# An S5 scan layer on one core: the last quarter's odd columns in VectorE's scan, its lag products and early halves ahead of the scan's end

## The chip, the cores and the metric

The kernel runs on one core of a Trainium2 chip. The metric is the device time of one execution in microseconds; three executions of the kernel before took 1019.77, 1023.63 and 1024.74 us, so the median is 1023.63 us. Engines are named as in the profile: PE is TensorE (PEld its weight loads), DVE is VectorE, ACT is ScalarE, POOL is GpSimd, SP is SyncE, which here only issues DMAs.

## The reference

One layer works on 1024 latent tokens and 256 context tokens of width 1024, all in fp32. The mixer is a bidirectional S5: 64 groups of 16 channels, each with 64 complex states per direction.

```python
def run(u, h0):
    bu = jnp.einsum('lgh,gnh->lgn', u.astype(F32), b_bar)
    bu = bu.at[0].add(lam_bar * h0)
    a = jnp.broadcast_to(lam_bar, bu.shape)
    _, h = lax.associative_scan(_linear_combine, (a, bu), axis=0)
    return jnp.einsum('lgn,ghn->lgh', h, c_mat).real, h[-1]
...
def out(y, h):
    y = y.reshape(h.shape).astype(h.dtype) + d_skip * h
    g = jax.nn.gelu(y)
    return g * jax.nn.sigmoid(g @ w_glu + b_glu)
...
x = x + m_l[2][:, None] * y_l
h_l = modulate(rms_norm(x, norm_ffn[i]), m_l[3][:, None], m_l[4][:, None])
x = x + m_l[5][:, None] * swiglu(h_l, ffn_w1[i], ffn_w3[i], ffn_w2[i])
return rms_norm(x, norm_final)
```

Forward and backward direction are summed. Norms, shifts, scales and gates surround the mixer and a SwiGLU FFN of hidden width 2816; the output is the latent stream.

## The kernel before, in words

**Chunks.** Tokens are cut into chunks of eight: 32 context chunks, then 128 latent ones. Per chunk PE sums the inputs into one state contribution (`sums`), so the recurrence runs over 160 columns. The states lie in the tile `ra` in four quarters `STQ[q]`; a quarter is `[160 columns, 2 (real, imaginary), 16]`, 20.125 KB per partition, and `STE` is all four seen as one. A quarter belongs to two units; unit k has eight groups, and `16 q + 8 (k % 2)` is its place among the states, four places for the forward direction and four for the backward one. Column 31 is the last context state, columns 32 to 159 are latent. "Early" is the first 64 latent chunks, "late" the rest.

**The scan** (line 839) is a chain on VectorE over all quarters at once. Its first loop takes 32 steps of two columns (32 odd columns of the early half), the second 63 steps of one column through the late half. A step is two products and two additions (lines 637 and 846), each addition reading what is just written. The even-numbered places of the early half that the first loop jumps over are filled in separately with one product pair and two additions (`rot_ops`): for quarters 0 and 2 by `fill_ops` on VectorE, one such instruction after each of the step's two additions (`one`), for quarters 1 and 3 by `fill` on POOL (`F10 F11` and `F30 F31`, 16 instructions each pair).

**What each unit needs on PE.** `k_mats` (K, two per quarter, line 802) multiplies lag by lag the kernels of chunk-internal inputs; two ACT copies and two ACT DMAs bring its result to DRAM (`KD_`). `toeplitz` (T, line 824) is a DMA from there, issued by SP, that lays the lags out as a matrix in `KQ`; unit k uses loads 2k and 2k+1, which need both K of the quarter. `x_mm` multiplies the unit's inputs with the two halves of that matrix (line 945). `states_mm` (line 914) multiplies the chunk-start states with C: forward states straight from `STQ`, backward ones from a turned copy (`turned`: R for the early half, Z for the late). For units 0 to 5, P does `x_mm` and the early half into PSUM, Y copies that into `Y` with ACT, and after the scan N does the late half, D adds it to `Y` on VectorE, H is the GELU on ACT. Units 6 and 7 are done whole behind the scan: z turns all 128 columns, Q does `x_mm` and `states_all` (line 925), and H reads PSUM.

**The order** is written out by hand in two strings, `PROG1` (its PSUM pools are those of the scan) and `PROG2` (a new pool of eight banks `pe8` that lies over all of them). Each word is an operation and a number, and `run` (line 954) emits them one after the other; each engine executes its instructions in this order. C is a product of C with powers of lambda on POOL, summed by POOL (`E` in `HOWS`, line 30) or by PE and an ACT copy (`P`, line 669). A is the adaLN product, I and J turn the mixer's output and split it into two fp32r parts for the GLU, W and V split GLU weights, g starts GLU products, w, l, b and m are DMA loads on SP. Behind `PROG2` come the GLU units, the FFN and the final norm, almost all of it PE work.

Of the kernel before, what the change touches and what calls it, by code (L numbers as in the profile page):

```python
# [10 lines left out]
F32 = mybir.dt.float32  # L11
# [6 lines left out]
P = 128  # L18
# [5 lines left out]
T = 8  # L24
# [2 lines left out]
NS = 64  # L27
EPS = 1e-6
MAGIC = 12582912.0
HOWS = "PPPP PPEE PEEE EEEE"  # L30
ZEN = "VVSVSVSV"
PROG1 = ("A22 B0 A26 C02 G1 A30 A34 C03 A40 K0 A44 A48 C10 K1 L2 A54 G2 C11 A60 F10 C12 F11 C13 T0 T1 T2 T3 A64 M0 M1 K2 R0 P0 Y0 Y1 K3 L3 R1 C20 P1 Y2 Y3 T4 T5 G3 T6 T7 C21 C22 C23 K4 R2 P2 Y4 Y5 K5 R3 P3 Y6 Y7 T8 T9 T10 T11 C30 C31 R4 P4 Y8 Y9 C32 C33 R5 P5 Y10 Y11 M2 m0 F30 F31")
# [10 lines left out]
def s5_ffn_kernel(tc, a, out):  # L43
# [3 lines left out]
    with ctx:  # L47
# [776 lines left out]
        def toeplitz(u):  # L824

            q, gi = divmod(u, 4)
            rows = KD_[q][32 * gi:32 * gi + HC]
            n = 15 * HC
            src = bass.AP(rows.tensor, rows.offset, [[HC, T], [n, 4 * HC], [1, P]])
            SY.dma_start(KQ[u % 4], src)  # L830
# [64 lines left out]
        def turned(k, half, hs, eng):  # L895

            e = 8 * (k % 2) + 4
            n = 128 if half == 2 else 64
            c1 = 94 if half == 0 else 158
            src = STQ[k // 2][:, c1:c1 - n:-1, :, e:e + 4]  # L900
            if eng is S:
                S.copy(hs, src)
# [6 lines left out]
        def yview(k, gp):  # L909
            return Y[:, k].rearrange("p t (a e h) -> p e a t h", e=2, h=HC)[:, gp]  # L910

        def states_mm(k, pts, half, hs, start):

            for a_ in range(4):
                for ri in range(2):
                    for d in range(2):
                        cs_ = slice(64 * (half ^ d), 64 * (half ^ d) + 64)
                        c0 = 31 + 64 * half
                        for gp in range(2):
                            ps = slice(64 * gp, 64 * gp + 64)  # L920
                            st = hs[ps, :, ri, a_] if d else STQ[k // 2][ps, c0:c0 + 64, ri, 8 * (k % 2) + a_]
                            PE.matmul(flat(pts[gp][cs_, a_]), st, flat(CL[k // 2][ps, ri, d, 4 * (k % 2) + a_]),
                                      start=start and ri == 0, stop=ri == 1 and (start or a_ == 3))

        def states_all(k, pts, hs):

            for a_ in range(4):
                for ri in range(2):
                    for d in range(2):
                        for c in range(2):  # L930
                            cs_ = slice(64 * c, 64 * c + 64)
                            for gp in range(2):
                                ps = slice(64 * gp, 64 * gp + 64)
                                st = hs[ps, cs_, ri, a_] if d else STQ[k // 2][ps, 31 + 64 * c:95 + 64 * c, ri, 8 * (k % 2) + a_]
                                PE.matmul(flat(pts[gp][cs_, a_]), st, flat(CL[k // 2][ps, ri, d, 4 * (k % 2) + a_]),
                                          start=False, stop=a_ + ri + d == 5)

        def x_mm(k, pool):

            pts = [pool([4, T, HC]) for _ in range(2)]  # L940
            for a_ in range(4):
                for gp in range(2):
                    g = 2 * a_ + gp
                    kq = KQ[(2 * k + g // 4) % 4][:, g % 4].rearrange("p (t h) -> p t h", t=T)[:, ::-1]
                    PE.matmul(pts[gp][:, a_], U[:, 8 * k + g, 32:160], kq, start=a_ == 0, stop=False)
            return pts

        scan()
        inner = {}
        HSe = [view(r, kb, [64, 2, 4]) for r, kb in ((RC[3], 14), (RC[3], 12), (RC[3], 14), (RC[3], 12), (RA, 2), (RA, 0))]  # L950
        HSl = [view(RA, STB * (i // 3) + 4.125 + 2 * (i % 3), [64, 2, 4]) for i in range(6)]
        HSq = {6: view(RA, 0, [P, 2, 4]), 7: view(RA, STB, [P, 2, 4])}

        def run(prog):


            for w in prog.split():
# [2 lines left out]
                    ada(i)  # L960
                elif op == "M":
                    mod_cols(i)
                elif op == "k":
                    KT[i] = [pe8([15 * HC]) for _ in range(2)]
                    for kv in KT[i]:
                        V.memset(kv, 0.0)
                elif op == "K":
                    k_mats(*divmod(i, 2), KT.get(i) or [kt, zeros(pw([15 * HC])) if i < 4 else pm[:, 0:15 * HC]])
                elif op == "L":
                    cs_load(i, S)  # L970
                elif op == "G":
# [6 lines left out]
                    for f in cl_ops(q, part, cts[q][part], HOW[q][part]):  # L978
                        f()
                elif op == "F":  # L980
                    fill(*divmod(i, 10), *((RW, 0) if i >= 30 else (RC[3], 12)))
                elif op == "T":
                    toeplitz(i)
                elif op == "R":
                    turned(i, 0, HSe[i], S)
                elif op == "Z":
                    turned(i, 1, HSl[i], ENG[ZEN[i]])
                elif op == "z":
                    turned(i, 2, HSq[i], ENG[ZEN[i]])
                elif op == "P":  # L990
                    inner[i] = x_mm(i, pw)
                    states_mm(i, inner[i], 0, HSe[i], False)
                elif op == "Q":
                    inner[i] = x_mm(i, pe8)
                    states_all(i, inner[i], HSq[i])
                elif op == "Y":
                    S.copy(yview(i // 2, i % 2), inner[i // 2][i % 2])
                elif op == "N":
# [3 lines left out]
                    for gp, po in enumerate(late[i]):  # L1002
                        tt(yview(i, gp), po, yview(i, gp), ADD)
                elif op == "H":
                    if i in late:
                        S.activation(Y[:, i], Y[:, i], AF.Gelu_apprx_tanh)
                    else:
                        for gp in range(2):
                            S.activation(yview(i, gp), inner[i][gp], AF.Gelu_apprx_tanh)
                elif op == "I":  # L1010
                    if GH[0] is None:
                        GH[0] = tuple(view(region(t, 16, R32), 0, [4, 8, P]) for t in ("c1", "c0"))
# [25 lines left out]
                elif op == "g":  # L1038
                    glu_mm(0, i // 10, range(i % 10 + 1))

        KT = {}
# [718 lines left out]
```

## Time and profile before

The profiled execution is the reference for every term; its own time is its span.

| what | value |
|---|---|
| times, three runs | 1019.77, 1023.63, 1024.74 us |
| profiled execution, span | 1023.7 us |
| PE busy | 964.6 us, 94% |
| DVE, POOL, ACT busy | 789.9, 766.2, 436.2 us |
| last step of the scan on DVE | begins at 230.08 us, 0.29 us long |
| last fill of POOL | begins at 235.13 us, 1.62 us for two |
| first GLU product on PE (g03) | 267.71 us |

A row of a timeline gives the start, the length, the engine, the line, the output and input tiles, how many equal instructions were merged, and in brackets how long the engine had been idle and what ended that. A row of the windows gives the stretch and its length, then busy time (and count) of PE, PEld, DVE, ACT and POOL, the granted PE clock as a share of full speed, and the DMA share and GB/s.

### The profile page before, as it was taken

The numbers are of one execution on the slowest core, as the hardware profiler recorded it, in microseconds if no ns is written. First come the engines' busy times: TensorE is split into PE (matmuls) and PEld (weight loads), VectorE is DVE, ScalarE is ACT, GpSimd is POOL, SyncE is SP. The second block draws the span as 40 slices with busy tenths as digits, with TensorE's granted clock in tenths as the row PEclk, the third lists the DMA queues.
The fourth block names the chain that finished last, engine by engine and source line by source line (L and its number), as shares of the span: only waits on it lengthen the run. The fifth ranks groups of instructions, "written<-read, shape, count | busy, mean of one in ns | idle before, by whom it ended". The sixth has DMA issues, their size and how long they took to land. (4 is left out here: it accounts for less than half of the span.)

```text
span 1023.7 us, 18545 instructions
## 1 busy us (share of the span) xinstructions
PE 964.6 (94%) x6988; PEld 774.7 (76%) x6988; DVE 789.9 (77%) x1642; ACT 436.2 (43%) x854; POOL 766.2 (75%) x590
## 2 busy tenths in 40 slices
PE   4987898878999999999999999999999999999996
PEld 1465523768999988877888888888888888888885
DVE  8889699995365778898867768595858778686977
ACT  4476722325353663523334343424334343423337
POOL 4699989992591458879787877778686877778674
PEclk9998999989999999999999999999999999999998
DMA  8865997322623021011212011121212112121205
GB/s 296 313 125 98 280 334 251 99 73 54 238 79 87 2 103 62 21 42 42 82 42 65 32 60 55 49 73 47 78 41 77 38 42 62 42 72 52 72 21 164
DMA packets 48545, 98.95 MB, mean 97 GB/s; under 512 B 4284, under 2 KB 18876, under 8 KB 47176
## 3 DMA queue, kind: packets, MB, share of 16 engines
q1 hardware_dynamic: 43272, 86.64, 25.8%
q0 software_dynamic: 2016, 7.34, 3.8%
q10 hardware_dynamic: 3168, 3.79, 1.1%
q8 instruction: 55, 0.90, 0.4%
q14 instruction: 34, 0.28, 0.1%
HBM read 84.25 MB, written 6.17 MB: 88 GB/s over the span
## 5 line engine op out<-in xcount | busy, mean ns | idle before, releaser
L77 POOL TENSOR_TENSOR c<-rxc,c 128x512 fp32r<-128x512 f32 x128 | 170.4, 1345 | 53.0 <-ACT c L1227 52.8
L1286 PE MATMUL ut<-ra,c 128*128 128x512 f32 x400 | 155.8, 389 | 1.0 <-ACT ra L1227 1.0
L1287 PE MATMUL ut<-ra,c 128*128 128x512 f32 x400 | 155.7, 389 | 0.3 <-DVE ra L77 0.3
L1288 PE MATMUL ut<-ra,c 128*128 128x512 f32 x400 | 155.6, 389 | 0.0
L1227 ACT CAST c<-rxc 128x512 fp32r<-128x512 f32 x128 | 78.9, 622 | 146.3 <-PE xt L1568 51.8
L1568 PE MATMUL xt<-c,c 128*128 128x512 f32 x540 | 129.7, 389 | 0.0
L1568 PEld LDWEIGHTS xt<-c,c 128*128 128x128 f32 x540 | 101.4, 188 | 21.0
L77 DVE TENSOR_TENSOR ru<-ru,xt 128x1024 f32<-128x1024 f32 x90 | 107.0, 1214 | 9.7 <-PE xt L1568 7.2
L77 DVE TENSOR_TENSOR ru<-ut,ru 128x512 f32<-128x512 f32 x98 | 67.1, 686 | 42.6 <-PE ut L1288 37.1
L1286 PEld LDWEIGHTS ut<-ra,c 128*128 128x128 f32 x400 | 75.1, 188 | 17.4 <-ACT ra L1227 1.4
L1287 PEld LDWEIGHTS ut<-ra,c 128*128 128x128 f32 x400 | 75.1, 188 | 16.2 <-issue 0.6
L1288 PEld LDWEIGHTS ut<-ra,c 128*128 128x128 f32 x400 | 75.1, 188 | 15.5
L77 POOL TENSOR_TENSOR c<-rw,c 128x512 fp32r<-128x512 f32 (+1 forms) x29 | 41.7, 1436 | 37.7 <-ACT c L1227 37.0
L1288 PE MATMUL ut<-c,c 128*128 128x512 f32 x160 | 62.4, 390 | 1.3 <-POOL c L77 1.3
L77 POOL TENSOR_TENSOR c<-ru,c 128x512 fp32r<-128x512 f32 (+1 forms) x39 | 55.4, 1420 | 9.3 <-ACT c L1227 4.9
L1286 PE MATMUL ut<-c,c 128*128 128x512 f32 x160 | 62.3, 389 | 0.0
L1287 PE MATMUL ut<-c,c 128*128 128x512 f32 x160 | 62.2, 389 | 0.0
L77 POOL TENSOR_TENSOR rxc<-rxc 128x512 f32<-128x512 f32 x40 | 60.6, 1516 | 1.6
L1568 PE MATMUL ut<-c,c 128*128 128x512 f32 x216 | 51.9, 389 | 0.0
L584 PE MATMUL pv<-ru,c 128*64 128x160 f32 x512 | 44.4, 316 | 7.6 <-POOL ru L77 2.8
L77 DVE TENSOR_TENSOR pe<-pe,ru 128x256 f32<-128x256 f32 x64 | 27.4, 429 | 29.5 <-ACT pe L1127 17.4
L77 DVE TENSOR_TENSOR ru<-ru,ut 128x512 f32<-128x512 f32 x76 | 47.2, 678 | 0.3
(446 smaller groups left out, 2581.8 us busy)
## 6 DMA issues: line engine op xcount, KB each, us to landing
c<-in_ada_w SPq DMA_DIRECT2D x46, 256.0 KB
rxc<-in_w SPq DMA_DIRECT2D x38, 256.0 KB
rxc<-in_w SPq DMA_DIRECT2D x19, 512.0 KB
ru<-in_w SPq DMA_DIRECT2D x11, 512.0 KB
rw<-in_w SPq DMA_DIRECT2D x11, 512.0 KB
ra<-in_ada_w SPq DMA_DIRECT2D x10, 512.0 KB
ra<-in_ada_w SPq DMA_DIRECT2D x18, 256.0 KB
ru<-in_xT SPq DMA_DIRECT2D x4, 1024.0 KB
```

The source lines that it names most:

```text
L77: eng.tensor_tensor(out=o, in0=x, in1=y, op=op)
L584: PE.matmul(pv[64 * (i % 2):64 * (i % 2) + 64, ri, c0:c0 + 160], w[:, i, 64 * ri:64 * ri + 64], U[:, 8 * b + 4 * j + i], start=True, stop= ...
L1227: S.copy(o[0], x)
L1286: PE.matmul(pu, wh, bh, start=start, stop=False)
L1287: PE.matmul(pu, wh, bl, start=False, stop=False)
L1288: PE.matmul(pu, wl, bh, start=False, stop=stop)
L1568: PE.matmul(pd, w[:, cs_], b, start=j in (1, 2, 4) and n == 0, stop=n == 2, skip_group_check=j not in (1, 2, 4))
```

## The change

The scan fills 28 groups of columns instead of 16 in its second part: quarter 2 as before, all of quarter 3's first eight places, and half of the other eight. What is left of quarter 3 is one call of `fill` with four POOL instructions (`f7`). One of quarter 3's C sums goes from POOL to PE (`HOWS`, `EEPE`). In `PROG1`, K5 stands directly behind K4, the loads T8 to T11 get places of their own (`KQ`), K6, K7 and T12 to T15 come ahead of the end, and units 6 and 7 get an early half: R6, `p6`, R7, `p7` (states first, then `x_mm`), and Y12 to Y15. Their late half then goes through Z, N and D as for the other units. The turned copies of units 2 to 7 (`HSe`) lie in rows of quarter 0 that are done with. The GLU weight loads w0, w1 and l1 and the bias load b0 move into `PROG1`. `states_all`, the full turning (`z`) and the K tiles of `PROG2` (`k`) go.

```diff
-HOWS = "PPPP PPEE PEEE EEEE"
+HOWS = "PPPP PPEE PEEE EEPE"
...
-PROG1 = ("... T6 T7 C21 C22 C23 K4 R2 P2 Y4 Y5 K5 R3 P3 Y6 Y7 T8 T9 T10 T11 C30 C31 R4 P4 Y8 Y9 C32 C33 R5 P5 Y10 Y11 M2 m0 F30 F31")
-PROG2 = ("k6 Z0 N0 Z1 Z2 D0 Z3 N1 k7 D1 Z4 H0 H1 K6 N2 D2 H2 K7 T12 T13 T14 T15 N3 Z5 D3 H3 N4 D4 z6 z7 I0 J0 I1 J1 w0 w1 l1 H4 N5 D5 I2 J2 H5 I3 J3 W0 W1 x0 x1 x2 x3"
-         " Q6 H6 I4 J4 Q7 b0 I5 J5 H7 g03 g13 I6 J6 g23 g05 g15 I7 J7 V1 w20 w21 g26 x10 x11 x12 x13")
+PROG1 = ("... T6 T7 C21 C22 C23 K4 K5 T8 T9 R2 P2 Y4 Y5 R3 P3 Y6 Y7 T10 T11"
+         " C30 C31 R4 P4 Y8 Y9 R5 P5 Y10 Y11 C32 C33 K6 K7 T12 T13 T14 T15 M2 m0 f7 w0 w1 l1 R6 p6 R7 p7 Y12 Y13 Y14 Y15 b0")
+PROG2 = ("Z0 Z1 Z2 N0 D0 Z3 N1 D1 Z4 H0 H1 N2 D2 H2 Z5 N3 D3 H3 Z6 N4 D4 Z7 I0 J0 I1 J1 H4 N5 D5 I2 J2 H5 I3 J3 W0 W1 x0 x1 x2 x3"
+         " N6 D6 H6 I4 J4 N7 D7 I5 J5 H7 g03 g13 I6 J6 g23 g05 g15 I7 J7 V1 w20 w21 g26 x10 x11 x12 x13")
...
-        KQ = [view(RA, STB * (2 + i // 2) + 2 * (i % 2), [4, P]) for i in range(4)]
+        KQ = [view(RA, STB * (2 + i // 2) + 2 * (i % 2), [4, P]) for i in range(4)] * 2
+        KQ += [view(RA, kb, [4, P]) for kb in (0, 2, STB + 4.125, STB + 6.125)] + KQ[:4]
...
-            for j in range(8):
-                for d in range(2):
-                    rest.extend(fill_ops(2, d, j))
+            for k in range(4, 8):
+                for j in range(4 if k == 7 else 8):
+                    rest.extend(fill_ops(k // 2, k % 2, j))
...
-        def fill(q, h, reg, kb):
+        def fill(q, h, reg, kb, es=(0, 8)):
...
-            for e in (0, 8):
+            for e in es:
...
-        def states_mm(k, pts, half, hs, start):
+        def states_mm(k, pts, half, hs, start, alone=True):
...
-                                      start=start and ri == 0, stop=ri == 1 and (start or a_ == 3))
+                                      start=start and ri == 0 and (alone or a_ == 0),
+                                      stop=alone and ri == 1 and (start or a_ == 3))
...
-        HSe = [view(r, kb, [64, 2, 4]) for r, kb in ((RC[3], 14), (RC[3], 12), (RC[3], 14), (RC[3], 12), (RA, 2), (RA, 0))]
-        HSl = [view(RA, STB * (i // 3) + 4.125 + 2 * (i % 3), [64, 2, 4]) for i in range(6)]
-        HSq = {6: view(RA, 0, [P, 2, 4]), 7: view(RA, STB, [P, 2, 4])}
+        HSe = [view(r, kb, [64, 2, 4]) for r, kb in [(RC[3], 14), (RC[3], 12)] + [(RA, 4.125 + 2 * j) for j in range(3)] * 2]
+        HSl = [view(RA, STB * (i // 3) + 4.125 + 2 * (i % 3), [64, 2, 4]) for i in range(8)]
...
+                elif op == "f":
+                    fill(i // 2, 1, RW, 0, (8 * (i % 2),))
...
+                elif op == "p":
+                    if i == 6:
+                        inner[i] = [pw([4, T, HC]) for _ in range(2)]
+                    else:
+                        inner[i] = [p_.tile([P, 4, T, HC], F32, tag=t, name="pi") for p_, t in ((pA, "r3"), (pW, "m"))]
+                    states_mm(i, inner[i], 0, HSe[i], True, False)
+                    x_mm(i, inner[i])
```

More of the change, by code (lines that the diff above doesn't have):

```diff
@@ L29 @@
 MAGIC = 12582912.0
-HOWS = "PPPP PPEE PEEE EEEE"
+HOWS = "PPPP PPEE PEEE EEPE"
 ZEN = "VVSVSVSV"
-PROG1 = ("A22 B0 A26 C02 G1 A30 A34 C03 A40 K0 A44 A48 C10 K1 L2 A54 G2 C11 A60 F10 C12 F11 C13 T0 T1 T2 T3 A64 M0 M1 K2 R0 P0 Y0 Y1 K3 L3 R1 C20 P1 Y2 Y3 T4 T5 G3 T6 T7 C21 C22 C23 K4 R2 P2 Y4 Y5 K5 R3 P3 Y6 Y7 T8 T9 T10 T11 C30 C31 R4 P4 Y8 Y9 C32 C33 R5 P5 Y10 Y11 M2 m0 F30 F31")
-PROG2 = ("k6 Z0 N0 Z1 Z2 D0 Z3 N1 k7 D1 Z4 H0 H1 K6 N2 D2 H2 K7 T12 T13 T14 T15 N3 Z5 D3 H3 N4 D4 z6 z7 I0 J0 I1 J1 w0 w1 l1 H4 N5 D5 I2 J2 H5 I3 J3 W0 W1 x0 x1 x2 x3"
-         " Q6 H6 I4 J4 Q7 b0 I5 J5 H7 g03 g13 I6 J6 g23 g05 g15 I7 J7 V1 w20 w21 g26 x10 x11 x12 x13")
+PROG1 = ("A22 B0 A26 C02 G1 A30 A34 C03 A40 K0 A44 A48 C10 K1 L2 A54 G2 C11 A60 F10 C12 F11 C13 T0 T1 T2 T3 A64 M0 M1 K2 R0 P0 Y0 Y1 K3 L3 R1 C20 P1 Y2 Y3 T4 T5 G3 T6 T7 C21 C22 C23 K4 K5 T8 T9 R2 P2 Y4 Y5 R3 P3 Y6 Y7 T10 T11"
+         " C30 C31 R4 P4 Y8 Y9 R5 P5 Y10 Y11 C32 C33 K6 K7 T12 T13 T14 T15 M2 m0 f7 w0 w1 l1 R6 p6 R7 p7 Y12 Y13 Y14 Y15 b0")
+PROG2 = ("Z0 Z1 Z2 N0 D0 Z3 N1 D1 Z4 H0 H1 N2 D2 H2 Z5 N3 D3 H3 Z6 N4 D4 Z7 I0 J0 I1 J1 H4 N5 D5 I2 J2 H5 I3 J3 W0 W1 x0 x1 x2 x3"
+         " N6 D6 H6 I4 J4 N7 D7 I5 J5 H7 g03 g13 I6 J6 g23 g05 g15 I7 J7 V1 w20 w21 g26 x10 x11 x12 x13")
 LOG2E = 1.4426950408889634
@@ L829, in toeplitz @@
             src = bass.AP(rows.tensor, rows.offset, [[HC, T], [n, 4 * HC], [1, P]])
-            SY.dma_start(KQ[u % 4], src)
+            SY.dma_start(KQ[u], src)
         def fill_ops(q, h, j):
@@ L897, in turned @@
             e = 8 * (k % 2) + 4
-            n = 128 if half == 2 else 64
-            c1 = 94 if half == 0 else 158
-            src = STQ[k // 2][:, c1:c1 - n:-1, :, e:e + 4]
+            c1 = 94 + 64 * half
+            src = STQ[k // 2][:, c1:c1 - 64:-1, :, e:e + 4]
             if eng is S:
@@ L922, in states_mm, with x_mm @@
                             PE.matmul(flat(pts[gp][cs_, a_]), st, flat(CL[k // 2][ps, ri, d, 4 * (k % 2) + a_]),
-                                      start=start and ri == 0, stop=ri == 1 and (start or a_ == 3))
[L925 to L940, printed above, removed]
+                                      start=start and ri == 0 and (alone or a_ == 0),
+                                      stop=alone and ri == 1 and (start or a_ == 3))
+        def x_mm(k, pts):
             for a_ in range(4):
@@ L943, in x_mm @@
                     g = 2 * a_ + gp
-                    kq = KQ[(2 * k + g // 4) % 4][:, g % 4].rearrange("p (t h) -> p t h", t=T)[:, ::-1]
-                    PE.matmul(pts[gp][:, a_], U[:, 8 * k + g, 32:160], kq, start=a_ == 0, stop=False)
-            return pts
+                    kq = KQ[2 * k + g // 4][:, g % 4].rearrange("p (t h) -> p t h", t=T)[:, ::-1]
+                    PE.matmul(pts[gp][:, a_], U[:, 8 * k + g, 32:160], kq, start=a_ == 0 and k < 6, stop=a_ == 3 and k > 5)
         scan()
         inner = {}
-        HSe = [view(r, kb, [64, 2, 4]) for r, kb in ((RC[3], 14), (RC[3], 12), (RC[3], 14), (RC[3], 12), (RA, 2), (RA, 0))]
-        HSl = [view(RA, STB * (i // 3) + 4.125 + 2 * (i % 3), [64, 2, 4]) for i in range(6)]
-        HSq = {6: view(RA, 0, [P, 2, 4]), 7: view(RA, STB, [P, 2, 4])}
+        HSe = [view(r, kb, [64, 2, 4]) for r, kb in [(RC[3], 14), (RC[3], 12)] + [(RA, 4.125 + 2 * j) for j in range(3)] * 2]
+        HSl = [view(RA, STB * (i // 3) + 4.125 + 2 * (i % 3), [64, 2, 4]) for i in range(8)]
         def run(prog):
@@ L962, in run @@
                     mod_cols(i)
[L963 to L966, printed above, removed]
                 elif op == "K":
-                    k_mats(*divmod(i, 2), KT.get(i) or [kt, zeros(pw([15 * HC])) if i < 4 else pm[:, 0:15 * HC]])
+                    k_mats(*divmod(i, 2), [kt, zeros(pw([15 * HC])) if i < 4 else pm[:, 0:15 * HC]])
                 elif op == "L":
@@ L980, in run @@
                 elif op == "F":
-                    fill(*divmod(i, 10), *((RW, 0) if i >= 30 else (RC[3], 12)))
+                    fill(*divmod(i, 10), RC[3], 12)
+                elif op == "f":
+                    fill(i // 2, 1, RW, 0, (8 * (i % 2),))
                 elif op == "T":
@@ L987, in run @@
                     turned(i, 1, HSl[i], ENG[ZEN[i]])
-                elif op == "z":
-                    turned(i, 2, HSq[i], ENG[ZEN[i]])
                 elif op == "P":
-                    inner[i] = x_mm(i, pw)
+                    inner[i] = [pw([4, T, HC]) for _ in range(2)]
+                    x_mm(i, inner[i])
                     states_mm(i, inner[i], 0, HSe[i], False)
-                elif op == "Q":
-                    inner[i] = x_mm(i, pe8)
-                    states_all(i, inner[i], HSq[i])
+                elif op == "p":
+                    if i == 6:
+                        inner[i] = [pw([4, T, HC]) for _ in range(2)]
+                    else:
+                        inner[i] = [p_.tile([P, 4, T, HC], F32, tag=t, name="pi") for p_, t in ((pA, "r3"), (pW, "m"))]
+                    states_mm(i, inner[i], 0, HSe[i], True, False)
+                    x_mm(i, inner[i])
                 elif op == "Y":
@@ L1004, in run @@
                 elif op == "H":
[L1005 to L1009, printed above, removed]
+                    S.activation(Y[:, i], Y[:, i], AF.Gelu_apprx_tanh)
                 elif op == "I":
@@ L1039, in run @@
                     glu_mm(0, i // 10, range(i % 10 + 1))
-        KT = {}
         late, W0, WR, PZ, GH, GR = {}, [], [], {}, [None, None], []
```

## The prediction

> **What bounds the kernel now.** I read the page first: the totals and the two rows in slices that matter.
>
> ```profile
> span 1023.7 us, 18545 instructions
> PE 964.6 (94%) x6988; PEld 774.7 (76%) x6988; DVE 789.9 (77%) x1642; ACT 436.2 (43%) x854; POOL 766.2 (75%) x590
> PE   4987898878999999999999999999999999999996
> PEclk9998999989999999999999999999999999999998
> ```
>
> PE is the bound of everything from the eleventh slice on, and has holes only in the first ten. So a change in the scan's neighbourhood is worth what it shifts the point from which PE runs without a hole. The busy time by windows gives that point.
>
> ```profile
> 227.50:230.50 3.00, 0.00 (x0) 0.02 (x1) 2.78 (x13) 1.17 (x3) 2.92 (x6) 1.00 0.00 0
> 230.50:267.70 37.20, 34.11 (x984) 32.21 (x985) 17.88 (x28) 14.42 (x21) 11.74 (x12) 0.95 0.41 130
> 267.70:320.00 52.30, 52.30 (x443) 52.30 (x442) 26.42 (x59) 26.02 (x64) 32.47 (x16) 1.00 0.37 120
> ```
>
> Before 230.5 PE stands for 3 us (DVE is finishing the scan), then 37.2 us of S5 remainder follow with 3.1 us of holes, and from the first GLU product at 267.7 on PE has none. The whole forecast is the time at which that first GLU product (g03) starts in the changed kernel; what follows it is the same work and moves with it. Next I read PE's timeline for prices and waits.
>
> ```profile
> 164.41 3.70 PE L672 MATMUL pw<-c,r 128*128 128x512 f32 x8
> 198.55 0.28 PE L809 MATMUL kt<-c,rxa 64*16 64x112 f32 x1 [2.23 <-POOL c L77]
> 205.41 0.27 PE L809 MATMUL kt<-c,rxa 64*16 64x112 f32 x1
> 206.92 0.17 PE L817 MATMUL pm<-rxc,rxa 64*16 64x16 f32 x1
> 207.02 2.05 PE L945 MATMUL pw<-ra,ru 128*128 128x128 f32 x16
> 215.08 1.44 PE L945 MATMUL pw<-ra,ru 128*128 128x128 f32 x8 [3.45 <-DMA ra<-kd]
> 217.11 2.08 PE L945 MATMUL pw<-ra,ru 128*128 128x128 f32 x8 [0.59 <-DMA ra<-kd]
> 222.69 0.49 PE L945 MATMUL pw<-ra,ru 128*128 128x128 f32 x2
> 223.46 1.83 PE L945 MATMUL pw<-ra,ru 128*128 128x128 f32 x14 [0.28 <-ACT ru L997]
> 225.22 2.27 PE L922 MATMUL pw<-c,ra 64*64 64x128 f32 x64
> 230.51 0.49 PE L922 MATMUL pe<-c,ra 64*64 64x128 f32 x4 [3.02 <-DVE ra L77]
> 253.08 1.09 PE L1056 MATMUL pe<-r,ru 128*128 128x128 f32 x8
> 267.71 0.36 PE L1097 MATMUL pe<-c,c 128*128 128x256 f32 x1
> ```
>
> Prices: a C sum on PE 3.7; a K 1.7 (205.41 to 207.09, K5); `x_mm` 2.05, each half 1.03; one half of the states 2.2 to the next start; an I 0.55 (two in 1.09). A P behind a P costs 4.8 (222.69 to 227.49), since its second PSUM tile waits 0.7 for the Y copy. The most important price is a wait: K5 ends at 207.09, and its lags come back from DRAM so that PE's first half can start at 215.08 and the second at 217.11, 8.0 and 10.0 us later. That trip passes ACT's queue and SP's:
>
> ```profile
> 201.32 0.36 ACT L821 COPY r<-pm 128x240 f32<-128x240 f32 x1 [0.40 <-ACT r L821]
> 208.29 0.37 ACTq L822 DMA_DIRECT2D kd<-rw  x1
> 212.62 0.63 ACT L902 COPY ra<-ra 128x512 f32<-128x512 f32 x1
> 222.82 1.07 ACT L997 COPY ru<-pw 128x512 f32<-128x512 f32 x2 [9.57 <-PE pw L922]
> 210.09 4.30 SPq L830 DMA_DIRECT2D ra<-kd  x4
> ```
>
> (The first of these belongs to K4, the others to K5, R4, Y8 with Y9, and T8 to T11.) No row of PE waits for such a trip behind the scan by more than 0.4, because other units' work lies over it.
>
> **The change part by part.** *The scan.* Rows of VectorE, one product of four successive steps, the scan's end, and a D:
>
> ```profile
> 201.11 0.29 DVE L77 TENSOR_TENSOR ltb<-ra,lta 128x128 f32<-128x128 f32 x1
> 202.17 0.29 DVE L77 TENSOR_TENSOR ltb<-ra,lta 128x128 f32<-128x128 f32 x1
> 203.20 0.29 DVE L77 TENSOR_TENSOR ltb<-ra,lta 128x128 f32<-128x128 f32 x1
> 204.25 0.30 DVE L77 TENSOR_TENSOR ltb<-ra,lta 128x128 f32<-128x128 f32 x1
> 230.08 0.29 DVE L77 TENSOR_TENSOR ra<-ltc,ra 128x128 f32<-128x128 f32 x1
> 247.62 1.29 DVE L77 TENSOR_TENSOR ru<-pe,ru 128x512 f32<-128x512 f32 x2 [3.63 <-PE pe L922]
> ```
>
> A step with two fill instructions takes 1.06, one without 1.05: an addition that needs the last result leaves a gap in which the fill lies. The second loop has 126 places; before, 8 left over from quarter 0 and 64 for quarter 2 use 72 of them, after, 8 and 28 times 4 make 120. So 48 instructions come in for 24 times 0.01 = 0.25 us. The cover is that gap; without it they would cost about 0.13 each, 6 us. Unit 6's places are complete after 104 slots (step 52, 219 us), unit 7's after 120 (step 60, 228 us).
>
> *POOL.* The first row is C32's sum, the next C33's; the last two are the first and the last pair of the 16 fills.
>
> ```profile
> 215.49 2.35 POOL L77 TENSOR_TENSOR c<-c,ra 128x1024 f32<-128x1024 f32 x1
> 221.88 2.36 POOL L77 TENSOR_TENSOR c<-c,rw 128x1024 f32<-128x1024 f32 x1
> 224.77 1.42 POOL L77 TENSOR_TENSOR rw<-ra,r 128x256 f32<-128x256 f32 x2
> 235.13 1.62 POOL L77 TENSOR_TENSOR ra<-ra,rw 128x256 f32<-128x256 f32 x2
> ```
>
> C32's sum (2.35) leaves, so C33 is done at 221.9 and the four fills of `f7` (3.0) about 225.5, instead of 236.75. Both are earlier than PE can use them, as follows.
>
> *PE up to K7.* K4 is as before (POOL releases its second part at 198.55). K5 now stands right behind it and needs K4's PSUM tiles, which ACT has copied at 201.68, 1.2 behind K4's end: K5 201.7 to 203.4. P2: 2.05 and 2.2, and 0.3 for R2, which stands behind K5's copies on ACT: 208.0. P3 and P4 4.8 each: 212.8 and 217.6 (T8, T9 land by 213.4, ten after K5, in time). T10 and T11 go into rows of quarter 1 that P3 still reads, so SP issues them at 213; from issue to PE the rows show 5.0 (210.09 to 215.08), so 218 and 220, and P5 ends at 220 + 1.03 + 2.2 = 223.2. C32 on PE: 226.9. K6: 228.6. K7 needs K6's tiles, copied 1.2 later: 229.8 to 231.5.
>
> *The trip for units 6 and 7.* T12 to T15 wait for K7. With the 8.0 and 2.0 a load, PE may start the four halves at 239.5, 241.5, 243.5 and 245.5. `p6` does its states first, from 233.7 (R6 stands behind K7's copies and DMAs on ACT) to 236, then waits 3.5 for T12: queued behind it on PE are p7 and every N, and the late halves wait for them. `x_mm` 6 ends at 242.5, states 7 at 244.7, `x_mm` 7 at 246.8. The first N needs the PSUM bank of unit 7's first half, copied by Y14 0.7 later: 247.5. What the scan's end (230.6) released before is then no longer what is late.
>
> *From there to g03.* Eight N at 2.2 and six I at 0.55 make 20.9: 268.4. D at 1.29 fits beside an N. Small waits: between nothing and the 3.1 of the window before; I take 0.8, as fewer dependences are tight: 269.2. D, Z, H and the GLU loads lie under PE here; the loads have been issued some 15 us earlier and are no term.
>
> *The clock.* Four rows of windows of 2 us:
>
> ```profile
> 200.00:202.00 2.00, 2.00 (x68) 1.96 (x57) 2.00 (x13) 0.72 (x2) 2.00 (x2) 0.50 0.20 62
> 218.00:220.00 2.00, 2.00 (x22) 1.78 (x25) 1.86 (x9) 0.00 (x0) 2.00 (x2) 0.50 0.50 123
> 234.00:236.00 2.00, 2.00 (x46) 2.00 (x43) 1.50 (x3) 0.18 (x1) 1.92 (x4) 0.50 0.00 0
> 238.00:240.00 2.00, 2.00 (x134) 1.97 (x121) 0.52 (x1) 1.31 (x2) 0.00 (x0) 1.00 0.04 8
> ```
>
> The granted clock is 0.50 after each of PE's waits of 2.23, 3.45 and 3.02 us quoted above. At that clock a half of `x_mm` takes 2.08 instead of 1.03. The changed kernel has waits of 2.2 (231.5 to 233.7), 3.5 and 1.0 at this place; between 239.5 and 246.8 lie 6.3 us of products, which would cost nothing more if the clock stays, and 6.3 if all run at half. I take 1.5, about what one half-clocked stretch of 3 us loses, as after the wait of 3.02. [...]
>
> **Sum.** g03 at 269.2 + 1.5 = 270.7 against 267.7, so 3.0 later: 1023.7 + 3.0 = 1026.7 us (1025.2 if the clock stays at full) for the profiled execution, whose span is within 0.1 us of the median of 1023.63, so no correction. What was taken from behind the scan (two K, two `x_mm`, two halves of states, 11.7 us of PE) comes back as PE waiting for the lags' way through DRAM.
>
> **The rivals.** *Faster: the trip is covered.* If the waits I put into K5 to K7 (1.2, 0.3, twice 0.7, 1.4 in P5, 1.2: 5.5 in all) vanish, K7 ends at 226.0, and with the clock at full the sum is 1025.2 - 5.5 = 1019.7; a part of the trip must go too. At the furthest N0 follows the scan's end by a turned copy, at 231.6, g03 is at 253.3, and the time 1009. For it: these waits are chained guesses, and PE had 3.45 idle at 211.6 that the new order uses. Against: each has its row, and PE's stream from K5 to K7 is 25.4 us of products alone. I give the case 1016, nearer to 1019.7 than to 1009.
>
> *Slower: the half clock holds through p6 and p7.* Place: PE from 239.5 to the first N. Price: up to 6.3 instead of 1.5, so 1026.7 + 4.8 = 1031.5. It decides once more than 3.6 us of these products' extra time is paid (1028.8). For it: the row at 218, where the clock was still 0.50 though PE had been at work again since 215.08. Against: behind the wait of 3.02 the clock was full again by 238.
>
> *No effect on the end at all* (the units' early halves wait for the fills): unit 7's states would have to start before 228; they start at 242.5, so this gets no chance of its own.
>
> **How the numbers follow.** A measurement of this kernel can tell about 0.5%, 5.1 us, from no change. The forecast case (1021 to 1028.7) gets 0.52, the faster rival 0.18, the slower one 0.30. The range takes the whole forecast case, the slower rival to 1033 (its 1031.5 and 1.5 of the small waits that I took as 0.8 of at most 3.1), and of the faster one the part from 1016 on. The forecast case's own range is 1021 to 1029. Faster by over 0.5% 0.18, within 0.52, slower 0.30.
>
> **What would show it.** Right: DVE's scan ends by 231 with no fill behind it; POOL's last fill of `ra` ends near 225.5; K7 near 231.5; rows of line 945 behind it wait for `ra<-kd`, over 2 us in sum; the first N starts near 247 behind ACT's line 997, not behind DVE; 0.50 stands in the clock there; g03 is near 270. Wrong: line 945 has no wait for `kd` behind K7, or the first N starts before 240; then the trip is not what is late, and the time is that of the faster rival. If g03 is where I say and the end isn't, the part behind it does not move as one.

## The result and the profile after

| kernel | median, us | range, us | executions | ratio to before (95% interval) |
|---|---|---|---|---|
| before | 1023.63 | 1019.77 to 1027.57 | 5 | |
| after | 1029.97 | 1028.45 to 1031.77 | 5 | 1.0058 [1.0042, 1.0075] |

The changed kernel is slower by 0.6%, 6.3 us from median to median; 1026.7 was forecast, in a range from 1016 to 1033. The profiled execution of after took 1029.19 us. First its page: span, PE's totals, PE and its clock in 40 slices.

```profile
span 1027.4 us, 18605 instructions
...
PE 968.1 (94%) x6996; PEld 776.1 (76%) x6996; DVE 791.1 (77%) x1690; ACT 440.3 (43%) x860; POOL 755.6 (74%) x577
...
PE   5987798797999999999999999999999999999996
...
PEclk9999999898999999999999999999999999999998
```

The span is 3.7 longer than before's, and PE is busy 3.5 longer. From the eleventh slice on it is as full as before, and from the first GLU product (g03) to the end of the span before takes 756.0 us and after 756.6. So nearly all of the difference arises ahead of g03. The windows of after show it: the two stretches that the prediction opened with, then K4 to K7, K7 to the first N, the first N to g03, and the whole.

```profile
227.50:230.50 3.00, 3.00 (x147) 1.96 (x146) 1.76 (x7) 0.96 (x2) 0.00 (x0) 1.00 0.02 5
230.50:267.70 37.20, 30.90 (x791) 28.24 (x778) 11.25 (x20) 15.84 (x24) 0.00 (x0) 0.91 0.42 129
...
196.94:234.09 37.15, 33.13 (x890) 27.68 (x890) 32.25 (x179) 9.78 (x20) 26.29 (x18) 0.83 0.21 52
234.09:251.05 16.96, 11.70 (x161) 10.38 (x161) 0.43 (x1) 3.57 (x8) 0.00 (x0) 0.80 0.65 181
251.05:270.84 19.79, 19.79 (x536) 18.80 (x537) 13.63 (x23) 11.86 (x16) 2.00 (x1) 1.00 0.19 75
196.94:270.84 73.90, 64.61 (x1584) 56.87 (x1585) 46.31 (x203) 25.21 (x43) 28.29 (x19) 0.87 0.30 88
```

The same stretch of before, from K4's second part (its seventeenth product, the one that waits for POOL; it is what "K4" stands for in these times) to g03:

```profile
198.55:267.71 69.16, 58.75 (x1576) 54.87 (x1577) 47.96 (x158) 22.52 (x37) 43.13 (x34) 0.90 0.35 105
```

PE's 3 us of standing still ahead of 230.5 are gone, as the change wants. But behind it PE is idle for 6.3 instead of 3.1. Over the whole stretch idle time falls from 10.41 to 9.29 only, and busy time grows by 5.86. With K4 1.61 earlier, g03 comes at 270.84 instead of 267.71, 3.13 later. PE's timeline of after, from K4 to g03:

```profile
196.94 0.36 PE L811 MATMUL kt<-c,rxa 64*16 64x112 f32 x1 [3.88 <-POOL c L78]
...
203.77 3.78 PE L933 MATMUL pw<-ra,ru 128*128 128x128 f32 x16 [1.15 <-issue]
...
220.07 1.44 PE L933 MATMUL pw<-ra,ru 128*128 128x128 f32 x8 [0.17 <-PE pw L923]
221.98 1.16 PE L933 MATMUL pw<-ra,ru 128*128 128x128 f32 x8 [0.47 <-DMA ra<-kd]
223.07 2.27 PE L923 MATMUL pw<-c,ra 64*64 64x128 f32 x64
225.27 1.12 PE L673 MATMUL pw<-c,r 128*128 128x512 f32 x2
...
231.16 0.36 PE L811 MATMUL kt<-c,rxa 64*16 64x112 f32 x2 [0.47 <-ACT r L823]
...
233.91 0.17 PE L819 MATMUL pm<-rxc,rxa 64*16 64x16 f32 x1
234.02 0.49 PE L923 MATMUL pw<-c,ra 64*64 64x128 f32 x4
236.38 1.98 PE L923 MATMUL pw<-c,ra 64*64 64x128 f32 x36 [1.88 <-ACT ra L903]
241.91 1.16 PE L933 MATMUL pw<-ra,ru 128*128 128x128 f32 x8 [2.06 <-DMA ra<-kd]
243.95 2.08 PE L933 MATMUL pw<-ra,ru 128*128 128x128 f32 x8 [0.88 <-DMA ra<-kd]
245.96 2.66 PE L923 MATMUL pi<-c,ra 64*64 64x128 f32 x64
248.54 2.05 PE L933 MATMUL pi<-ra,ru 128*128 128x128 f32 x16
251.05 1.21 PE L923 MATMUL pe<-c,ra 64*64 64x128 f32 x30 [0.45 <-ACT ru L984]
...
270.84 0.36 PE L1079 MATMUL pe<-c,c 128*128 128x256 f32 x1
271.59 0.39 PE L1080 MATMUL pe<-c,c 128*128 128x256 f32 x1 [0.39 <-POOL c L78]
```

L811 to L819 are a K, L933 is `x_mm`, L923 the states, L673 the C sum, `pe<-c,ra` on L923 an N. K7 ends at 234.08; then the states of unit 6 wait for their turned copy (ACT L903), `x_mm` 6 waits twice for the lags, and everything of unit 7 and all N stand behind. VectorE meanwhile: the scan's last addition, the first Z behind it, and then nothing for 10.46 us until PE has finished with `ra`.

```profile
228.65 0.29 DVE L78 TENSOR_TENSOR ra<-ltc,ra 128x128 f32<-128x128 f32 x1
229.07 0.43 DVE L905 COPY ra<-ra 128x512 f32<-128x512 f32 x1
239.96 0.43 DVE L905 COPY ra<-ra 128x512 f32<-128x512 f32 x1 [10.46 <-PE pw L923]
```

POOL's last two fills, and its next work:

```profile
222.09 1.55 POOL L78 TENSOR_TENSOR ra<-ra,rw 128x256 f32<-128x256 f32 x2
268.84 2.70 POOL L78 TENSOR_TENSOR c<-rxa,c 128x1024 fp32r<-128x1024 f32 x1 [45.20 <-DVE c L1057]
```

Windows of 2 us of after for the clock (the column before the last two):

```profile
204.00:206.00 2.00, 2.00 (x10) 2.00 (x11) 2.00 (x12) 0.62 (x1) 2.00 (x2) 0.50 0.36 112
...
238.00:240.00 2.00, 1.85 (x32) 1.45 (x24) 0.04 (x1) 0.00 (x0) 0.00 (x0) 0.50 0.33 66
240.00:242.00 2.00, 0.09 (x1) 0.09 (x1) 0.39 (x1) 0.00 (x0) 0.00 (x0) 0.93 0.60 137
...
244.00:246.00 2.00, 2.00 (x12) 1.77 (x12) 0.00 (x0) 0.36 (x1) 0.00 (x0) 0.50 0.94 206
```

At half clock run three stretches: 13.7 us from 195.9, 3.4 from 236.8 and 3.4 from 243.7.

### The profile page after: what moved, and what is told of

Its sections match the earlier page's. It is cut to its first block, busy times and chain, and to the rows that moved or that the text cites. A ratio compares the mean times of both kernels' runs of the same rounds, so it can differ in the third digit from the quotient of the medians.

```text
span 1027.4 us, 18605 instructions
## 1 busy us (share of the span) xinstructions
PE 968.1 (94%) x6996; PEld 776.1 (76%) x6996; DVE 791.1 (77%) x1690; ACT 440.3 (43%) x860; POOL 755.6 (74%) x577
## 5 line engine op out<-in xcount | busy, mean ns | idle before, releaser
L78 POOL TENSOR_TENSOR c<-rxa,c 128x512 fp32r<-128x512 f32 (+1 forms) x5 | 7.9, 1574 | 59.1 <-DVE c L1057 45.2
```

What stands on the lines that cost most here:

```text
L78: eng.tensor_tensor(out=o, in0=x, in1=y, op=op)
```

## The experiments

The theory: the loss is the way of unit 6's and 7's lags through DRAM, paid because `p6` and `p7` stand between K7 and the first N. Against it stood: C32's 3.7 us on PE; the long half-clocked stretch ahead of K7; and that POOL or the scan is what matters. Each row is the median of 5 to 11 executions beside executions of the kernel before on the same chip (median there 1023.63 to 1024.32). The trace of a kernel is one of its executions: that of e8 is 5.0 us above its median, those of e2 and e12 are 4.8 and 2.7 below theirs.

| kernel | what is different | median, us | ratio to before |
|---|---|---|---|
| after | | 1029.97 | 1.0058 [1.0042, 1.0075] |
| e1 | after, no trip for the last lags | 1025.34 | 1.0010 [0.9993, 1.0028] |
| e2 | after, C32's sum on POOL | 1027.12 | 1.0019 [1.0000, 1.0038] |
| e3 | after, `x_mm` of 6 and 7 behind N | 1025.69 | 1.0014 [0.9997, 1.0031] |
| e4 | e3, early states ahead of K6 and K7 | 1025.17 | 1.0005 [0.9987, 1.0024] |
| e5 | e4, C32's sum on POOL | 1022.10 | 0.9969 [0.9954, 0.9984] |
| e7 | after, units 6 and 7 whole and late | 1023.33 | 0.9988 [0.9979, 0.9997] |
| e8 | e7, C32's sum on POOL | 1018.98 | 0.9946 [0.9933, 0.9959] |
| e9 | before, the scan's part alone | 1023.57 | 0.9994 [0.9985, 1.0002] |
| e10 | after, 28 products ahead of K4 | 1030.38 | 1.0058 [1.0046, 1.0070] |
| e11 | after, 14 products ahead of K4 | 1031.02 | 1.0063 [1.0047, 1.0078] |
| e12 | e8, 14 products ahead of K4 | 1019.00 | 0.9944 [0.9926, 0.9963] |
| e14 | e5, 14 products ahead of K4 | 1019.81 | 0.9955 [0.9938, 0.9972] |

**e1, the trip taken away.** Units 6 and 7 use the lags of units 4 and 5, so its output is not that of the layer.

```diff
-... C32 C33 K6 K7 T12 T13 T14 T15 M2 m0 ...
+... C32 C33 K6 K7 M2 m0 ...
-        KQ += [view(RA, kb, [4, P]) for kb in (0, 2, STB + 4.125, STB + 6.125)] + KQ[:4]
+        KQ += [view(RA, kb, [4, P]) for kb in (0, 2, STB + 4.125, STB + 6.125)]
+        KQ += KQ[8:12]
```

> The changed kernel without the loads T12 to T15: units 6 and 7 multiply their inputs with the lags of units 4 and 5, which have long landed; K6 and K7 are still computed and written to DRAM. So the waits on the way through DRAM are gone and all of PE's work stays. Theory (the trip is what is late): x_mm 6 follows the states of unit 6 at once, no wait for kd; the first N starts 4.3 us earlier than the changed kernel's 251.05, g03 near 266.5, time about 4.3 us below the changed kernel. Rival (the half clock costs the time): the first N moves by 1.5 us at most. Rival (PE has simply more to do before the first N): no change.

4.6 us less than after. PE's timeline of e1 behind K7 (L924 are the states, L934 `x_mm`):

```profile
236.94 2.25 PE L924 MATMUL pw<-c,ra 64*64 64x128 f32 x60 [1.88 <-ACT ra L904]
239.13 2.05 PE L934 MATMUL pw<-ra,ru 128*128 128x128 f32 x16
...
245.80 0.41 PE L924 MATMUL pe<-c,ra 64*64 64x128 f32 x4 [0.45 <-ACT ru L985]
```

The wait for the turned copy is still 1.88; the two for the lags are gone, the clock stays full there, and the first N starts 5.25 earlier, which is more than either rival allowed (1.5 at most, and nothing).

**e3, the trip covered.** `x_mm` of units 6 and 7 goes behind their late states.

```diff
-                    states_mm(i, inner[i], 0, HSe[i], True, False)
-                    x_mm(i, inner[i])
+                    states_mm(i, inner[i], 0, HSe[i], True)
...
-                    states_mm(i, late[i], 1, HSl[i], True)
+                    states_mm(i, late[i], 1, HSl[i], True, i < 6)
+                    if i > 5:
+                        x_mm(i, late[i])
```

> The changed kernel with x_mm of units 6 and 7 in their late pass (N6, N7) instead of p6 and p7; the early half holds states alone, unit 7's early output rests in rows of quarter 0, b0 behind N7. The same work on PE, but six N lie over the trip. Theory: no wait for kd; states 6 from 236.4, states 7 to 242.1, first N near 242.8 instead of 251.05, g03 at 242.8 + 19.8 + 4.1 = 266.7, 4 us below the changed kernel. Rival (half clock): 1.5 us at most. Rival (work): no change.

4.3 us less, with the same work and the real lags. Both runs give the trip, with the half clock that follows its waits, as 4 to 5 of the 6.3 us.

**e2, C32's sum back on POOL.**

```diff
-HOWS = "PPPP PPEE PEEE EEPE"
+HOWS = "PPPP PPEE PEEE EEEE"
```

> The changed kernel with C32 summed by POOL again (HOWS ends EEEE). Theory (PE's chain up to K7 and then the trip): POOL is done with C33 near 222.5, before P5 ends at 225.3, so K6 starts 3.6 us earlier than 228.9 and everything behind it, g03 and the time moves by about 3.6 us. Rival (scan's end or POOL holds the first N): under 1 us, or slower, since POOL gets 2.35 us more.

2.9 us less than after; the same edit takes 3.1 from e4 (e5) and 4.4 from e7 (e8). So the sum's 3.7 us of PE are paid nearly in full wherever it is.

**e9, the scan's part alone**, put into the kernel before:

```diff
-            for j in range(8):
-                for d in range(2):
-                    rest.extend(fill_ops(2, d, j))
+            for k in range(4, 8):
+                for j in range(4 if k == 7 else 8):
+                    rest.extend(fill_ops(k // 2, k % 2, j))
...
-... M2 m0 F30 F31
+... M2 m0 f7
```

> The scan's part of the change alone in the kernel before: quarter 3's fills are put into the scan's gaps on VectorE, POOL keeps four of the sixteen fill instructions, and nothing else is changed. Theory (the fills lie in gaps of the scan, and nobody waits for POOL's fills in the kernel before): the scan's end moves by 0.3 us at most, POOL's last fill comes some 9 us earlier, and the time is within 1 us of the kernel before. Rival (units 6 and 7 wait for POOL): faster by 2 us or more.

No difference is seen (0.3 us less, the interval holds 1). In the kernel before, the scan's part by itself neither costs nor gains anything that these runs can tell.

**e7 and e8, the lag products alone.** K6, K7 and T12 to T15 stay ahead of the scan's end, the early halves of units 6 and 7 go; `states_all`, z and Q are those of the kernel before.

```diff
-... K6 K7 T12 T13 T14 T15 M2 m0 f7 w0 w1 l1 R6 p6 R7 p7 Y12 Y13 Y14 Y15 b0")
+... K6 K7 T12 T13 T14 T15 M2 m0 f7 w0 w1 l1")
-PROG2 = ("Z0 ... Z5 N3 D3 H3 Z6 N4 D4 Z7 I0 ... N6 D6 H6 I4 J4 N7 D7 I5 ...
+PROG2 = ("Z0 ... Z5 N3 D3 H3 N4 D4 z6 z7 I0 ... Q6 H6 I4 J4 Q7 b0 I5 ...
```

> One part of the change alone: the lag products K6 and K7 and the loads T12 to T15 stand ahead of the scan's end, but units 6 and 7 get no early half; they are done whole behind N5, as in the kernel before. Theory (PE pays for the trip of the lags only because p6 and p7 stand between K7 and the first N): with nothing of units 6 and 7 ahead of N0, K7 ends near 234 as in the changed kernel, the first N starts near 235 instead of 251.05, the trip lies under eight to ten us of late halves, no row of x_mm waits for the lags, and the first GLU product is near 263 instead of 270.8: some 7.5 us less than the changed kernel (about 1022.5) and 1 to 5 less than the kernel before. Rival (what is lost is PE's slow stretch from 196 to 234, whatever follows): the time stays within 2 us of the changed kernel's 1029.97.

> The kernel of e7_lags_alone with C32's sum back on POOL, so that PE's 3.7 us for it go and K6 waits for POOL instead, which then ends C33 near 224. Theory: K7 ends near 230.5, the first N is bound by the scan's end and its turned copy near 231.5, and the first GLU product comes near 259.5: 3.5 us less than e7_lags_alone, about 11 less than the changed kernel and 5 to 8 less than the kernel before. Rival (PE's instruction loads of 128 products each bind where narrow products stand close together, as in e4_states_first, where four of them left holes of 0.9 to 1.3 us): one or two more holes of about 1 us, and only 1.5 to 2.5 us less than e7_lags_alone.

e7 is 6.6 us below after: its K7 ends at 234.57, and the first N starts at 235.04 instead of 251.05. PE's waits in e7 from 228 to 275 (what waits, for what, us in total, times, longest) have none for `kd`:

```profile
PE pe L924 <- issue: 1.1, 1, 1.1
PE pe L947 <- issue: 0.8, 1, 0.8
PE kt L811 <- ACT r L823: 0.5, 1, 0.5
PE pe L924 <- ACT rw L823: 0.5, 1, 0.5
PE pm L811 <- ACT r L823: 0.5, 1, 0.5
PE pm L811 <- issue: 0.3, 1, 0.3
```

g03 is at 265.09 (263 expected, with holes of 1.14 and 0.80 that the profile calls "issue"). The rival is out. e8 is another 4.4 below, and beats both kernels: 0.5% below before, 1.1% below after.

**e4 and e5, early states ahead of the lag products.**

```diff
-... Y10 Y11 C32 C33 K6 K7 T12 T13 T14 T15 M2 m0 f7 w0 w1 l1 R6 p6 R7 p7 Y12 Y13 Y14 Y15
+... Y10 Y11 R6 C32 C33 M2 m0 f7 R7 p6 Y12 Y13 K6 p7 Y14 Y15 K7 T12 T13 T14 T15 w0 w1 l1
```

> As e3, and the early states of units 6 and 7 ahead of K6 and K7 (R6 before C32, R7 behind it, p6 and Y ahead of K6, p7 between K6 and K7), so that they lie over ACT's copies. Theory: p6 at 229, K6 to 232.8, p7 to 235, K7 to 236.7, first N at 237.3, T12 lands at 244.7 and N6 is due at 251.7: no wait; g03 near 261.2, about 9.5 us below the changed kernel and 6 below the one before. Rivals: what e3 gives, since N0 would not be held by this chain.

> The kernel of e4_states_first with C32's sum back on POOL. By PE's chain alone its first N comes 3.7 us earlier (near 236) and the time is 3.7 us less than e4_states_first (near 1021.5). Rival (PE's instruction loads bind there): holes of about 1 us stay behind each 128 products, and only 1 to 2.5 us are won.

e4 missed by half: 4.8 below after instead of 9.5, although no wait for the lags of units 6 and 7 stood ahead of the first N, which came at 239.74 (237.3 expected). The trace shows what took the rest: four waits of PE without a releaser, 4.2 us of the 4.7 that are missing.

```profile
233.92 0.17 PE L819 MATMUL kt<-rxc,rxa 64*16 64x16 f32 x1 [0.88 <-issue]
...
238.02 0.27 PE L811 MATMUL kt<-c,rxa 64*16 64x112 f32 x1 [0.90 <-issue]
...
241.86 9.68 PE L925 MATMUL pe<-c,ra 64*64 64x128 f32 x300 [1.15 <-issue]
...
257.45 0.77 PE L925 MATMUL pe<-c,ra 64*64 64x128 f32 x17 [1.25 <-issue]
```

What they seem to wait for is in the trace's DMA records: the queue that the page calls "q8 instruction" brings 16384 bytes at a time, and each hole follows such a load and lies at the same place of every 128 products (counted from the program's start, modulo 128; some records are missing):

```
kernel   load landed   PE went on   hole   product, mod 128
before     240.30        241.51     1.00      70
before     243.65        244.97     1.12      70
e4         232.64        233.92     0.88      69
e4         236.53        238.02     0.90      69
e4         240.34        241.86     1.15      68
e4         255.98        257.45     1.25      67
e8         243.20        244.67     2.52      70
e11        232.66        234.04     1.47      70
```

PE goes on 1.2 to 1.5 us behind the landing. In all fourteen profiles every wait of PE between 190 and 275 us that is called "issue" and lasts 0.4 us or more lies at products 67 to 72 of the 128. Where the products are narrow or short (K and states, 128 of them in 3 to 4 us), PE uses its instructions up faster than they come, as I read the table; in after, its other waits lay over that, but for the 1.15 ahead of P2 (at product 72, 1.36 behind a landing at 202.41). The pages of before and after count 55 such loads for 6988 and 6996 products and as many weight loads, about 254 instructions to a load, which agrees with 128 products and their weight loads. e5 gained 3.1 on e4, between the 3.7 of PE's chain and the rival's 2.5, and holes of up to 2.0 stayed in its trace: each theory holds in part.

**e10, e11, e12 and e14, the clock.** Products without use stand where PE waits for POOL ahead of K4, so that it isn't idle.

```diff
-... C21 C22 C23 K4 K5 T8 T9 ...
+... C21 C22 C23 d14 K4 K5 T8 T9 ...
...
+                elif op == "d":
+                    for _ in range(i):
+                        PE.matmul(kt[:, 0:P], U[:, 0, 32:160], U[:, 1, 32:160], start=True, stop=True)
```

> The changed kernel with 28 products of 128x128 by 128 columns (0.128 us each, 3.6 us) put on PE ahead of K4, where it waits 3.9 us for POOL; their result is written over. First theory (PE's idle stretch ahead of K4 is what halves the clock): the half-clocked stretch of 13.7 us from 196 goes, x_mm of P2 takes 2.05 us instead of 3.78, K7 ends near 231.5 instead of 234.1, and the time is 2 to 3 us less than the changed kernel's. Second theory (the narrow products of K4 and K5, 64x16, count as idleness for the clock): the half clock is still granted from about 200 on and the time is within 1 us of the changed kernel's.

> The changed kernel with 14 products ahead of K4 instead of the 28 of e10_busy_before_K4, whose 56 rows took 6.52 us and so put K4 off by 3.9 us; 14 should take 3.3 us and fit into PE's wait for POOL. Theory (the half clock after that wait costs the stretch K4 to P2 about 3.5 us, since in e10_busy_before_K4 K4 began 3.9 us later and P2 still ended at the same 210.7): K4 starts at 197, no half clock before 230, P2 ends near 207, K7 ends near 230.5 instead of 234.1, the first N starts near 247.5 instead of 251, and the time is 3 to 4 us less than the changed kernel's, so near 1026.5, about what the prediction gave. Rival (the lags' trip or POOL, not the clock, sets K7 and what follows): the time stays within 1 us of 1030.

In the profiles of both, and of e12 and e14, no half clock is granted between 196 and 230; in the eight kernels with this order and without the products it is there for 10.2 to 13.7 us. So PE's idleness ahead of K4 is what brings it on, not the narrow products of K4 and K5. But the time did not fall: 1030.38 and 1031.02. In e10 a product took two rows of 0.12, twice what I had reckoned, and K4 started 3.9 late. In e11 K4 started at 199.0 and K6 ended at 228.59, 2.1 ahead of after. There it was lost again; PE of e11 behind K6:

```profile
229.06 0.36 PE L811 MATMUL kt<-c,rxa 64*16 64x112 f32 x2 [0.47 <-ACT r L823]
...
234.04 0.20 PE L819 MATMUL pm<-rxc,rxa 64*16 64x16 f32 x1 [1.47 <-issue]
234.22 0.69 PE L923 MATMUL pw<-c,ra 64*64 64x128 f32 x4
237.85 3.59 PE L923 MATMUL pw<-c,ra 64*64 64x128 f32 x60 [2.94 <-ACT ra L903]
```

And its ACT queue:

```profile
235.53 1.61 ACTq L824 DMA_DIRECT2D kd<-rw  x1
237.18 1.14 ACT L903 COPY ra<-ra 128x512 f32<-128x512 f32 x2 [1.68 <-issue]
```

K7 has a hole of 1.47, which ends 1.38 behind the landing of an instruction load (232.66), and the DMA of its last tile is issued in 1.61 instead of 0.33 (another instruction load runs from 235.26 to 236.77; that it is the cause wasn't tried). R6, the lags and the first N (253.68) are later than in after. My theory, that filling the wait wins 3 to 4 us, fell: what sets the end is K7's last tile and the trip behind it. The half clock also came back: behind 230 it is granted for 17.1 us in e11 and 10.2 in e10, against 6.8 in after. How much of the time each of these takes, no run separates.

> The kernel of e8_lags_alone_pool with the 14 products ahead of K4. There the first N started at 231.72, right behind K7, while the scan's last row on VectorE ended at 229.82 and its turned copy was out at 230.7. Theory: K7 ends near 228, the first N is released by the turned copy near 230.5, so 1.2 us less than e8_lags_alone_pool (near 1017.8), and no more, as the scan is then the bound. Rival (the half clock costs more than K7's place): 3 us less or more.

> The kernel of e5_states_first_pool with the 14 products ahead of K4: the early halves of units 6 and 7 take room that the full clock makes ahead of the scan's end. Theory: K7 ends near 231, the first N starts near 231.7, the first GLU product comes near 258, and the time is about 12 us less than the changed kernel's, near 1017, level with or 1 us below e12_lags_alone_pool_busy. Rival (unit 7's early half waits for POOL's fills and the states until 228 and holds back K7 and all N): first N at 234 or later, and slower than e12_lags_alone_pool_busy by 2 us.

In e12's profiled execution K7 ended at 226.97 and the first N started at 228.16, released by the scan's last addition, which ended at 228.02; the turned copy, which the theory had as the release, starts at 228.15. From K4 to g03 PE ran at full clock:

```profile
195.74:258.30 62.56, 54.13 (x1594) 49.77 (x1594) 46.33 (x203) 22.55 (x37) 38.59 (x26) 1.00 0.41 119
```

That execution is the fastest of e12's six. The median of e12 is that of e8 (1019.00 and 1018.98): the 1.2 us weren't won on average. e14 is at 1019.81, 2.8 above what I expected and level with the two within the intervals: its first N comes at 235.74, as late as the rival had it. POOL's fills hold PE for only 0.6. The profile names K7's copies on ACT for the 2.1 ahead of the first N, but the first of them is out at 234.07; PE goes on at product 68, 1.34 behind an instruction load that landed at 234.40. So about 0.5 of this wait is the copy, and the rest bears the signs of the load.

e12's row is a measure for the others, since before has the same products between K4 and g03, and after has C32's 3.7 more. The row above takes in the first sixteen products of K4 and 0.1 us of g03, which those of before and after don't; between the seventeenth (196.07) and g03's start (258.20) e12's PE is busy for 53.7. So at full clock before's products take an estimated 53.7 and after's 57.4, and half clock took 58.75 - 53.7 = 5.0 in before's profile and 64.6 - 57.4 = 7.2 in after's. That closes the sum at g03: 1.6 earlier at K4, 3.7 for the sum on PE, 2.2 more half clock, 1.1 less idle: 3.2 later, 3.13 seen.

## Why the prediction was right, and by how much it was off

**Mechanism: right; the range, in part luck.** PE's stream behind the scan sets the end, and what the change takes ahead of the scan's end comes back as the wait for the lags; e1, e3 and e7 show it. But the median, 1029.97, lies above the forecast case's own range (1021 to 1029) and above the 1028.8 from which the slower rival was to be the answer. The stated range holds it only because that rival was taken in, and the rival's price was not paid, as the clock below shows. The outcome, slower by over 0.5%, had been given 0.30.

**Scan and POOL: right.** VectorE's last step begins at 228.65 (by 231 expected) with no fill behind it; POOL's last fill ends at 223.6 (225.5 expected). e9 shows no time in either.

**PE up to K7: 231.5 expected, 234.1 measured.** This term was mis-sized by more than the 2.6, as K4 came 1.61 earlier than assumed: from K4 to K7's end 32.95 were expected and 37.15 measured. P2 ran at half clock (`x_mm` 3.78, states 2.96 to the next start, instead of 2.05 and 2.2), with 1.15 of "issue" ahead of it, where an instruction load landed. K4 and K5 took 0.8 more. K7 took 2.9 instead of 1.7, with ACT's copies inside it, and started 0.5 behind K6 instead of 1.2. The 0.7 that the prediction takes for the wait of a P's second tile is 0.28 in the row it shows; in after it is 0.25, and a P behind a P takes 4.70, not 4.8.

**The trip: right.** K7's end to the first half of `x_mm` 6: 7.8 (8.0 expected); to the second 9.9 (10.0). The turned copy released `p6` 2.3 behind K7 (2.2 expected).

**First N: 247.5 expected, 251.05 measured**, behind ACT's L984 as said. Of the 3.55, 2.6 come from K7; the rest is the half clock, which the prediction's sum adds apart.

**From the first N to g03: 21.7 expected, 19.8 measured.** The first five N follow each other by 2.03, not 2.2, the six I took 3.05 instead of 3.3, and there were none of the small waits (0.8).

**Clock: 1.5 expected behind 239.5, about 1.4 measured** (second half of `x_mm` 6 2.08 instead of 1.03, states of unit 7 2.58 to the next start instead of 2.2). The slower rival needed over 3.6 there, so it isn't what happened, though the median is nearer to its 1031.5 than to 1026.7. The half clock from 236.85 came after a wait of 1.88 us, shorter than the 2.23, 3.45 and 3.02 that the prediction quotes. The clock of after changes only at points 3.41 us apart: of the steps between them PE, at work again from 203.77 on, fills the one from 206.13 to 209.54 (3.41 busy, against 2.06, 2.97 and 2.36 in the three ahead of it), and the clock rises at its end.

**g03: 270.7 expected, 270.84 measured. That they agree is luck.** K4 came 1.6 earlier, K4 to K7 took 4.2 more, K7 to the first N 0.5 less (half clock included), and the first N to g03 1.9 less.

**The profiled execution as the typical one: this step failed.** The prediction took before's span, within 0.1 us of the median, for its time and made no correction. But an execution's time is its span and 1.8 us (1029.19 and 1027.4 of after). So before's profiled execution took about 1025.5, 1.9 above its median, while after's lay 0.8 below its own. From span to span the change is 3.7 (3.0 expected; 0.4 of the rest is g03's second product waiting for POOL), and 3.7 + 1.9 + 0.8 are the 6.3 of the medians, but for rounding. Where before's 1.9 lie can be read at the start of the traces, where nothing was changed: ACT gets the last part of the inputs (`in_ctxT`) at 22.06 us in before's profile, and at 19.21 to 20.68 in the thirteen others; PE's first product of line 584 (a line or so lower in the others) starts at 41.82, against 39.92 to 40.44. The row of K4 quoted above, at 198.55 in before, lies at 195.73 to 197.80 in the nine others whose program is the same up to there. So the reference had lost 1.4 to 1.9 us ahead of 42 us that no other profiled execution lost, and this is also why K4 comes 1.61 earlier in after. (e9, whose median is that of before, has g03 at 264.95 in its profile instead of 267.71.) Why the inputs came later there stays open, and so does after's 0.8.

## What to carry to other kernels

Before moving work ahead of a serial chain, look at what its last product has to go through before it can be used: here ACT's copy, a DMA to DRAM and one back, 8 us, which must lie under work that needs none of it. Move the producers (e8: lag products early, users late), and don't put the users between them and the work that was ready. And put the profile's span on the scale of the runs before adding to it: it is one execution, here 1.9 us off its median where a change of 3.0 was forecast. A second trace, compared at an instruction ahead of the change, shows such an offset.

## What the runs showed of the hardware that was not expected

PE's instructions come in loads of 16384 bytes, by the count on the page (55 loads) some 128 products with their weight loads. Where that many took 3 to 4 us, PE stood still for up to 2.52 us at many of the boundaries; the profile mostly names it "issue". At the hole of 2.52 in e8 the load began at 241.99, only 0.16 before PE had nothing left, and the DMA engines were at a share of 1.0; that the one delayed the other was not tried.

In all fourteen profiles the granted clock changes only at points 3.41 us apart (after: 195.89, 209.54, 236.85, 240.26, 243.68, 247.09), so a half-clocked stretch lasts one such step or several, up to 13.7 us. A step need not be idle throughout to bring half clock on: in the steps of after that end at 195.89, 236.85 and 243.68, where the clock falls, PE is busy for 0.57, 1.53 and 1.16 us; in those that end at 209.54, 240.26 and 247.09, where it rises, for 3.41, 3.00 and 3.14. So how a wait lies across the steps counts as well as its length: the wait of 1.88 us for unit 6's turned copy lies in one step of after and halves the clock, and in e1, where a step ends in its middle (235.99), it does not.
